# Linear attention for both halves of a supertile in one go, two PSUM tiles in other banks, and another DMA rate in the planner

## The chip, the cores and the metric

One Trainium2 chip, one of its cores. The metric is the device time of one execution in microseconds (us). TensorE is called PE here, VectorE DVE, ScalarE ACT, GpSimd POOL and SyncE SP, as in the profile.

## The reference

One decoder layer on 4096 tokens of width 1024: a modulated RMSNorm gives h, one projection of h feeds three kinds of heads (banded attention, RWKV-7, gated linear attention), their gated outputs go through one output projection, a second norm and the residual. The change touches the linear attention:

```python
def _gla_mixer(h, q, k, v, gk1, gk2, gk_b, norm_w):
    gk = jax.nn.log_sigmoid(((h @ gk1) @ gk2 + gk_b).astype(f32)) / GLA_GATE_NORMALIZER
    ...
    def step(S, inp):
        q_c, k_c, v_c, g_c = inp
        b = jnp.cumsum(g_c, axis=2)
        diff = b[:, :, :, None, :] - b[:, :, None, :, :]
        diff = jnp.where(causal[:, :, None], diff, -jnp.inf)
        A = jnp.einsum('bhid,bhjd,bhijd->bhij', q_c, k_c, jnp.exp(diff))
        o = A @ v_c + jnp.einsum('bhid,bhdv->bhiv', q_c * jnp.exp(b), S)
        b_last = b[:, :, -1:, :]
        S = (jnp.exp(b_last[:, :, 0, :])[..., None] * S
             + jnp.einsum('bhjd,bhjv->bhdv', k_c * jnp.exp(b_last - b), v_c))
        return S, o
    ...
    o = o * lax.rsqrt(jnp.mean(o * o, axis=-1, keepdims=True) + 1e-5) * norm_w.astype(f32)
```

There are 4 heads with keys of 32 and values of 64.

## The kernel before, in words

The tokens are cut into 16 supertiles of 256 (NT), each of two halves of 128 (a = 0, 1). Part one runs norm, RWKV-7 and linear attention over all supertiles and prepares the weights of part two; part two runs banded attention and the output projection.

Part one is written as streams of Python generators, one per stage and supertile: a (norm; xh are tokens by row, xt by column, rb the transposed row scales, hT the result in two f16 parts), p (projections pv, lp, zz, gqk), d (gates; here called w; its running sums of log decays are cw), qa, qb, qc (the 64-blocks' triangular inverse), v, k (transposes kp of the keys, copied to BK), q2 (the serial RWKV recurrence: rp, up, sp, yp in four steps per supertile, then yt), r (linear attention), c, g and l (weights: squares, scales, splits into two f16 parts; cs and ch).

Every instruction is also noted by `Order.note`. When a part has been emitted, `Order.pin` plays the instructions through its own table of costs, engine by engine, and chains each engine's instructions in the order that comes out. So a cost in that table, a buffer or a bank that an instruction must wait for, and a joint burst (matmuls noted as one group) all move instructions of every engine. On PE the planner prefers a ready matmul of the same array tile size. A load's end is set by its size class or, if later, by a pipe that moves 310 GB/s.

PSUM has eight banks of 128 x 512 f32: pj twice (projections), and one each of m, mq, at, tr, y and sq. `pst(tag, name)` takes a bank; a new tile in it waits for the readers of the last. In part one mq serves ktp, gap, kvp and ot of stage r, kp of stage k, and most of qa, qc and v; at serves atp, one half of np, bp and gap, and op; tr serves rb, aps and one cw; m serves the gates and the other cw.

Stage r per supertile: POOL spreads q over heads (qb, two tiles, one per half), PE transposes k (ktp, copied to kt by ACT). Then for each half: gap (keys by queries, 4 matmuls in array tiles of 64*64 into two banks), and DVE masks it back into qb. Then for each half: Gst, the state spread over heads, from the packed state Gpk (DVE), kvp (keys by values, 4 matmuls in tiles of 128*32), the next Gpk (two DVE instructions), op (state by queries, 2 matmuls, and masked products by values, 8, in tiles of 128*64), and ACT copies op to osb. Last a norm per head (squares in osq), transposes ot and a store.

Of the kernel before, what the change touches and what calls it, by code (L numbers as in the profile page):

```python
# [16 lines left out]
ALU = mybir.AluOpType  # L17
# [4 lines left out]
P = 128  # L22
D = 1024
T = 4096
NT = 256
NS = T // NT
KD = D // P
HD = 64
# [5 lines left out]
LIFT = {}  # L34
LAG = {"l": 150}
URGENT = 150
TILING_WAIT = 0.6
LANES = ((0.06, 1.04e-3, VL), (0.02, 1.0e-3, AL), (0.1, 2.3e-3, 0.0), (0.0, 1e-3 / 2.4, PL), (0.05, 0.0, 2.0))

# [24 lines left out]
class Order:  # L64
# [157 lines left out]
    def pin(self):  # L222
# [4 lines left out]
        for k, st in enumerate(steps):  # L227
            if st.eng == "PE":
                h = head[k - 1] if k else 0
# [13 lines left out]
        cells, mode, table, pipe, half = [0.0] * 16, None, None, 0.0, {}  # L243
        last, count = {}, 0
        while count < len(steps):
            e = min((e for e in ENGINES if ready[e]), key=lambda e: max(free[e], min(ready[e].values())))
            now = max(free[e], min(ready[e].values())) + 1e-9
            at = sorted((k for k, t in ready[e].items() if t <= now), key=lambda k: (steps[k].rank, k))
            k = at[0]
            if e == "PE" and mode is not None and steps[k].array[0] != mode:  # L250

                same = [q for q in at if steps[q].array[0] == mode]
                wait = max(now - ready[e][q] for q in at if steps[q].array[0] != mode)
                if same and (mode != (4, 4) or wait < TILING_WAIT):
                    k = same[0]
            first = max(free[e], ready[e].pop(k))
            for k in bursts.get(k, [k]):
                st, t = steps[k], max(first, free[e])
                if e == "PE":
                    m, at, passes, took, issue = st.array  # L260
                    if mode is not None and m != mode:
                        t = max(t, max(cells)) + 0.094
                    mode = m
                    t = max(t, max(cells[c] for c in at))
                    for c in at:
                        cells[c] = t + passes * took
                    free[e], st.end = t + issue * passes, t + passes * took + 0.165
                else:
                    if st.half is not None:
                        was, half[e] = half.get(e, st.half), st.half  # L270
                        if was[0] != st.half[0] or None not in (was[1], st.half[1]) and was[1] != st.half[1]:
                            t = max(t, free[e] + 0.115)
                    if st.table is not None and st.table != table:
                        t, table = max(t, free[e] + 1.28), st.table
                    free[e], st.end = t + st.occ, t + st.lat
                    if st.bytes:

                        pipe = max(pipe, t + 1.7) + st.bytes / 310e3
                        st.end = max(st.end, pipe)
                st.start = t  # L280
                if e in last:
                    self.tc.add_manual_dep(
                        st.ins, last[e], mybir.DependencyInfo(mybir.DependencyClass.NoSync, mybir.DependencyReason.DATA))
                last[e], count = st.ins.name, count + 1
                for q in st.then:
                    to, h = steps[q], head[q]
                    left[h] -= 1
                    at = t if k in to.turn else 0.0
                    if k in to.needs and e != to.eng:
                        at = max(at, st.end + HOP_FROM[e] + HOP_INTO.get(to.eng, 0.0))  # L290
                    elif k in to.needs and (e == "SP" or e != "PE" and to.needs[k]):
                        at = max(at, st.end + (0.05 if e == "SP" else 0.03))
                    when[h] = max(when[h], at)
                    if not left[h]:
                        ready[to.eng][h] = when[h]
# [105 lines left out]
def hybrid_kernel(ctx, tc, x, xc, rows, ada1, adaw, w1, wl, w2, wo, cst, abias, out):  # L401
# [72 lines left out]

    ps = pool_of(ctx, "ps", 1, space=PSUM)

    def pst(tag, name, bufs=1):
        bufs = 2 if tag == "pj" else bufs
        t = ps.tile([P, 512], F32, tag=tag, name=name, bufs=bufs)
        model.take(tag, bufs, t.tensor.name)  # L480
        return t
# [7 lines left out]
    def mq(name):  # L489
        return pst("mq", name)  # L490
# [45 lines left out]
    def joint(on=True):  # L536
        model.order.joint = next(burst) if on else 0
# [102 lines left out]
    with ExitStack() as p1:  # L640
# [1 line left out]
        soon = ("tables", "scolb", "uw", "w0p0", "w0p1", "one16", "mu_s", "mu_c", "a0h")  # L642
        late = ("td", "tf0", "tf1", "Sst0", "Sst1", "lnx")
        tags = ("gvh", "gvl", "xh", "b1", "gl", "bl", "cs", "ch", "gw", "zs", "gaw", "gacc", "zl0", "zl1", "zl2", "early",
                "zb1", "ta", "em", "ep", "zb0", "b2", "zb2", "kg", "kt", "egm", "egp", "qg", "vg", "c2", "middle",
                "AS", "osb", "c3", "KB", "ATm", "c1", "RA", "UV", "BK", "cd", "em0", "bon", "ysb", "rs", "Ss", "lasts")
        wk1 = {n: pool_of(p1, f"work1{n}", 1) for n in tags}

# [6 lines left out]
        def wt(shape, name, bufs=1, dt=F32, tag=None):  # L655
            tag = tag or name
            return wk1[tag].tile(shape, dt, tag=tag, name=name, bufs=bufs)
# [5 lines left out]
            return wt(shape, name, 3, dt, "b1")  # L663

        def cs2(shape, name, dt=F32):
            return wt(shape, name, 2, dt, "c2")

        def cs1(shape, name, dt=F32):
            return wt(shape, name, 4, dt, "c1")
# [708 lines left out]
        def stage_r(i):  # L1378
# [2 lines left out]
            yield [("p", i), ("r", i - 1)]  # L1381
            qg, kg, vg, egp, egm = e["qg"], e["kg"], e["vg"], e["egp"], e["egm"]
            half = (slice(0, 64), slice(64, 128))
            qb = [cs2([P, 4, P], "qb") for _ in range(2)]
            for a in range(2):
                G.tensor_tensor(qb[a], qg[:, a, :].rearrange("p (o n) -> p o n", o=1).to_broadcast([P, 4, P]),
                                bdm.rearrange("p (h n) -> p h n", h=4)[:, :, 0:1].to_broadcast([P, 4, P]), op=ALU.mult)
            yield [kg, "mq"]
            ktp = mq("ktp")
# [1 line left out]
                PE.transpose(ktp[:, a * P : (a + 1) * P], kg[:, a, :], ident)  # L1391
            kt = wt([P, 2, P], "kt", 1)
            S.copy(kt.rearrange("p a n -> p (a n)"), ktp[:, :NT])
            for a in range(2):
                yield [qb[a], "at", "mq"]
                gap = [pst(tag, "gap")[:, 0:NT] for tag in ("at", "mq")]
                joint()
                for hk in half:
                    for hp, sl in enumerate(half):
                        PE.matmul(gap[hp][hk], kg[sl, a, hk], qb[a][sl, 2 * hp : 2 * hp + 2, :].rearrange("p h n -> p (h n)"),  # L1400
                                  start=True, stop=True)
                joint(False)

                for hp in range(2):
                    V.tensor_tensor(qb[a][:, 2 * hp : 2 * hp + 2, :], gap[hp].rearrange("p (h n) -> p h n", h=2),
                                    gmask.rearrange("p (o n) -> p o n", o=1).to_broadcast([P, 2, P]), op=ALU.mult)
            yield [kt, "mq"]
            osb = wt([P, 2, NT], "osb", 1)
            for a in range(2):
                gidx = 2 * i + a  # L1410
                Gc, now, then = Gst[gidx % 2], Gpk[gidx % 2], Gpk[(gidx + 1) % 2]
                heads4 = [t.rearrange("p (h n) -> p h n", h=4) for t in (Gc, bdm)]
                V.scalar_tensor_tensor(heads4[0], now.rearrange("p (o n) -> p o n", o=1).to_broadcast([P, 4, HD]),
                                       egm[:, a, 0:1], heads4[1], op0=ALU.mult, op1=ALU.mult)
                kvp = mq("kvp")
                joint()
                for h in range(4):
                    PE.matmul(kvp[32 * h : 32 * h + 32, 0:HD], kt[:, a, 32 * h : 32 * h + 32], vg[:, a, h * HD : h * HD + HD],
                              start=True, stop=True)
                joint(False)  # L1420
                V.scalar_tensor_tensor(then, now, egm[:, a, 0:1], kvp[:, 0:HD], op0=ALU.mult, op1=ALU.add)
                V.tensor_scalar(then, then, egp[:, a, 128:129], None, op0=ALU.mult)
                yield [Gc, qb[a], "at"]
                op_ = pst("at", "op")
                joint()
                for ht in half:
                    PE.matmul(op_[ht, :NT], qg[:, a, ht], Gc, start=True, stop=False)
                for h in range(4):
                    for ht in half:
                        PE.matmul(op_[ht, h * 64 : h * 64 + 64], qb[a][:, h, ht], vg[:, a, h * 64 : h * 64 + 64],  # L1430
                                  start=False, stop=(h == 3))
                joint(False)
                S.copy(osb[:, a, :], op_[:, :NT])
                yield [then, "mq"]
            osq = cs2([P, 2, NT], "osq")
            gla_norm(osb, osq)
            yield [osb, "mq"]

# [126 lines left out]
                    (8, "a", stage_a, i), (9, "c", stage_c, i), (10, "p", stage_p, i))  # L1565
        emit()
        model.order.pin()


    def pool2(name):  # L1570
# [664 lines left out]
```

## Time and profile before

| | |
|---|---|
| median of 3 runs | 2021.44 us (2020.94 to 2027.34) |
| the profiled execution | 2023.94 us, span 2022.1 us |
| granted PE clock, mean | 0.989 |
| PE / DVE / ACT / POOL busy | 1919.5 / 1506.7 / 1130.1 / 311.3 us |
| part one | to about 1050 us: the last yt starts at 1038.4 us |
| part two | from 961.8 us (its first projection, kp from hT), beside the end of part one |

A row of the profile gives the line, engine, operation, out<-in by tile names and shapes. Nearly all rows read L336, the helper that issues and notes every instruction, so tiles tell them apart. A timeline row begins with start and duration; the bracket at its end is the engine's idle time before it and what released it. In a tile's view the three durations are smallest, median and largest in ns, and below them come two lists: what the tile's engine waited for, and who waited for the tile (us, times).

### The profile page before, as it was taken

Reading aid. Unit: us, or ns where it says so; the run is one execution under the profiler, and the core shown is the slowest. Engines: PE = TensorE matmul, PEld = TensorE weight load, DVE = VectorE, ACT = ScalarE, POOL = GpSimd, SP = SyncE. Lnnn points to the kernel's source line nnn. Section 1 sums busy time; section 2 is a strip of 40 time slices with the busy share of each in tenths; the row PEclk is TensorE's granted clock in tenths of the full one; section 3 lists DMA queues with packets and bytes.
Section 4 is the critical chain, followed back from the end, with each engine's and each line's share of the span. In section 5 each row is a group of like instructions: output and inputs, shape, how many; then the busy total and the mean of one; then the engine's idle time right before and its main releaser. Section 6 shows DMA issues by size and latency. Waiting matters only on the chain.

```text
span 2022.1 us, 59931 instructions
## 1 busy us (share of the span) xinstructions
PE 1919.5 (95%) x24899; PEld 1483.7 (73%) x24899; DVE 1506.7 (75%) x4246; ACT 1130.1 (56%) x2609; POOL 311.3 (15%) x485
## 2 busy tenths in 40 slices
PE   5899999999999999999989999999999999999997
PEld 1677787777787777877767678877778777787683
DVE  5777877887778887776758876777767777676866
ACT  5878778765866765555434544444454444444443
POOL 0622213262221222221100000000000000000001
PEclk8899999999999999999999999999999999999998
DMA  9464535353424411124243433344333443334414
GB/s 373 150 208 148 164 114 160 118 150 110 131 76 147 151 37 60 61 76 141 93 152 125 154 106 117 117 139 139 97 108 116 149 129 112 110 108 141 128 36 168
DMA packets 154267, 258.77 MB, mean 128 GB/s; under 512 B 49026, under 2 KB 100738, under 8 KB 147716
## 3 DMA queue, kind: packets, MB, share of 16 engines
q1 hardware_dynamic: 153844, 254.34, 38.8%
q8 instruction: 198, 3.24, 0.6%
q14 instruction: 81, 0.66, 0.1%
q10 hardware_dynamic: 144, 0.52, 0.1%
HBM read 193.98 MB, written 60.82 MB: 126 GB/s over the span
## 4 chain that ended last, share of the span: by engine, by line
PE 54%; DVE 22%; ACT 9%; DMA 8%; issue 4%; SPq 2%; POOL 1%; DVEq 0%; ACTq 0%; POOLq 0%
PE gp L336 16%; PE op L336 12%; PE zz L336 4%; PE qp L336 3%; PE pv L336 2%; PE lp L336 2%; PE kp L336 2%; PE sc L336 2%; DVE pr L336 2%; PE ovp L336 2%; DVE q L336 2%; DVE mtp L336 2%; SPq L336 2%; DMA cs<-in_wo 1%; DVE tsc L336 1%
## 5 line engine op out<-in xcount | busy, mean ns | idle before, releaser
L336 PEld LDWEIGHTS <-mtp 128*128 128x128 f16 x1344 | 130.7, 98 | 146.0 <-issue 6.3
L336 PE MATMUL op<-o,mtp 128*128 128x512 f16 x768 | 172.9, 380 | 0.0
L336 ACT ACTIVATE pr<-pr,nm,lsc 128x256 f32<-128x256 f32 (+1 forms) x256 | 149.0, 584 | 11.5 <-DVE nm L336 11.4
L336 PE MATMUL op<-ov,mtp 128*128 128x512 f16 x576 | 144.0, 381 | 3.6 <-DMA ov<-woscr 3.5
L336 PEld LDWEIGHTS <-hT 128*128 128x128 f16 x1536 | 120.5, 100 | 24.5 <-issue 3.9
L336 ACT ACTIVATE mtp<-yv,oi 128x1024 f16<-128x1024 f32 x30 | 34.5, 1149 | 155.1 <-DVE yv L336 114.4
L336 DVE CUSTOM_DVE_ANT_0 pr<-sc,ab,kept 128x256 f32<-128x256 f32 (+1 forms) x256 | 108.4, 475 | 15.5 <-PE sc L336 15.2
L336 POOL TENSOR_TENSOR ry<-sy,expo 128x1 f32<-128x1 f32 x30 | 19.1, 638 | 588.3 <-DVE sy L336 588.3
L336 PE MATMUL pv<-gvh,hT 128*128 128x272 f16 x512 | 101.0, 290 | 5.6 <-ACT hT L336 2.6
L336 DVE TENSOR_TENSOR yv<-op,yv 128x512 f32<-128x512 f32 x105 | 70.3, 681 | 47.3 <-PE op L336 33.4
L336 DVE SCALAR_TENSOR_TENSOR ag<-ag,gp 128x512 f32<-128x512 f32 x64 | 43.4, 678 | 67.8 <-ACT ag L336 67.7
L336 PE MATMUL zz<-hT,rh 128*128 128x256 f16 x512 | 91.8, 277 | 1.7 <-DVE x L336 1.7
L336 PE MATMUL lp<-hT,Lh 128*128 128x256 f16 x512 | 91.3, 274 | 1.7 <-issue 1.6
L336 PE MATMUL zz<-hT,kh 128*128 128x256 f16 x512 | 91.9, 273 | 0.0
L336 ACT ACTIVATE ag<-gp,gh 128x512 f32<-128x512 f32 x64 | 43.9, 686 | 83.3 <-PE gp L336 83.3
L336 PE MATMUL qp<-hT,q1h 128*128 128x256 f16 x512 | 86.3, 273 | 3.7 <-DVE kT L336 3.7
L336 PE MATMUL zz<-hT,vh 128*128 128x256 f16 x512 | 89.4, 275 | 0.0
L336 PE MATMUL gqk<-hT,gqkh 128*128 128x256 f16 x512 | 87.5, 273 | 1.1 <-DVE zb L336 1.1
L336 PE MATMUL gp<-hT,q5h 128*128 128x256 f16 x512 | 86.3, 273 | 0.0
L336 PE MATMUL qp<-hT,q0h 128*128 128x256 f16 x512 | 85.4, 273 | 0.0
L336 PE MATMUL gp<-hT,q3h 128*128 128x256 f16 x512 | 85.3, 273 | 0.0
L336 PE MATMUL gp<-hT,q6h 128*128 128x256 f16 x512 | 85.2, 273 | 0.0
(442 smaller groups left out, 5858.5 us busy)
## 6 DMA issues: line engine op xcount, KB each, us to landing
ov<-woscr SPq DMA_DIRECT2D x96, 512.0 KB, 4.5
xh<-in_x SPq DMA_DIRECT2D x32, 512.0 KB, 4.2
xt<-in_xc SPq DMA_DIRECT2D x16, 1024.0 KB, 8.3
hscr<-hT SPq DMA_DIRECT2D x16, 1024.0 KB, 5.0
hT<-hscr SPq DMA_DIRECT2D x16, 1024.0 KB, 4.8
x<-in_x SPq DMA_DIRECT2D x30, 512.0 KB, 4.3
out<-yv SPq DMA_DIRECT2D x30, 512.0 KB, 3.0
cs<-in_w SPq DMA_DIRECT2D x56, 256.0 KB, 3.5
```

Of the source, the lines that this page charges most:

```text
L336: r = f(*args, **kw)
```

## The change

Three edits. First, stage r treats both halves together: one qb tile, gap as one burst of 8 matmuls into two banks and two masks of 128x512 for both halves, kvp as one burst of 8, then the two state updates on DVE, then op as one burst of 20 in one bank and one copy to osb. Second, in part one kp takes the bank tr instead of mq, and the cw that took m takes at. Third, the planner's pipe moves 400 GB/s instead of 310. The buffers of the tag c2 go from two to one, and osq has a tag of its own.

```diff
+HOME = {('kp', 'mq'): 'tr', ('cw', 'm'): 'at'}
...
-                        pipe = max(pipe, t + 1.7) + st.bytes / 310e3
+                        pipe = max(pipe, t + 1.7) + st.bytes / 400e3
...
+    first_phase = [True]
+
     def pst(tag, name, bufs=1):
+        tag = HOME.get((name, tag), tag) if first_phase else tag
...
         def cs2(shape, name, dt=F32):
-            return wt(shape, name, 2, dt, "c2")
+            return wt(shape, name, 1, dt, "c2")
...
-            qb = [cs2([P, 4, P], "qb") for _ in range(2)]
+            qb = cs2([P, 2, 4, P], "qb")
...
+            yield [qb, "at", "mq"]
+            gap = [pst(tag, "gap").rearrange("p (a n) -> p a n", a=2) for tag in ("at", "mq")]
+            joint()
             for a in range(2):
-                yield [qb[a], "at", "mq"]
-                gap = [pst(tag, "gap")[:, 0:NT] for tag in ("at", "mq")]
-                joint()
                 for hk in half:
                     for hp, sl in enumerate(half):
-                        PE.matmul(gap[hp][hk], kg[sl, a, hk], qb[a][sl, 2 * hp : 2 * hp + 2, :].rearrange("p h n -> p (h n)"),
+                        PE.matmul(gap[hp][hk, a], kg[sl, a, hk], qb[sl, a, 2 * hp : 2 * hp + 2, :].rearrange("p h n -> p (h n)"),
                                   start=True, stop=True)
-                joint(False)
-
-                for hp in range(2):
-                    V.tensor_tensor(qb[a][:, 2 * hp : 2 * hp + 2, :], gap[hp].rearrange("p (h n) -> p h n", h=2),
-                                    gmask.rearrange("p (o n) -> p o n", o=1).to_broadcast([P, 2, P]), op=ALU.mult)
+            joint(False)
+            for hp in range(2):
+                V.tensor_tensor(qb[:, :, 2 * hp : 2 * hp + 2, :], gap[hp].rearrange("p a (h n) -> p a h n", h=2),
+                                gmask.rearrange("p (a o n) -> p a o n", a=1, o=1).to_broadcast([P, 2, 2, P]), op=ALU.mult)
             yield [kt, "mq"]
+            kvp = mq("kvp")[:, 0 : 2 * HD].rearrange("p (a n) -> p a n", a=2)
+            joint()
+            for a in range(2):
+                for h in range(4):
+                    PE.matmul(kvp[32 * h : 32 * h + 32, a], kt[:, a, 32 * h : 32 * h + 32], vg[:, a, h * HD : h * HD + HD],
+                              start=True, stop=True)
+            joint(False)
...
-                V.scalar_tensor_tensor(then, now, egm[:, a, 0:1], kvp[:, 0:HD], op0=ALU.mult, op1=ALU.add)
+                V.scalar_tensor_tensor(then, now, egm[:, a, 0:1], kvp[:, a], op0=ALU.mult, op1=ALU.add)
                 V.tensor_scalar(then, then, egp[:, a, 128:129], None, op0=ALU.mult)
-                yield [Gc, qb[a], "at"]
-                op_ = pst("at", "op")
-                joint()
+            yield [*Gst, qb, "at"]
+            op_ = pst("at", "op").rearrange("p (a n) -> p a n", a=2)
+            joint()
+            for a in range(2):
                 for ht in half:
-                    PE.matmul(op_[ht, :NT], qg[:, a, ht], Gc, start=True, stop=False)
+                    PE.matmul(op_[ht, a], qg[:, a, ht], Gst[(2 * i + a) % 2], start=(a == 0), stop=False)
...
-                S.copy(osb[:, a, :], op_[:, :NT])
-                yield [then, "mq"]
-            osq = cs2([P, 2, NT], "osq")
+            joint(False)
+            S.copy(osb, op_)
+            osq = wt([P, 2, NT], "osq")
...
         model.order.pin()
+        first_phase.clear()
```

How the order of PE moves at stage r. Before, in the ninth supertile, around the second half's kvp and op (up, sp and yp are the recurrence, zz a projection):

```order
L336 MATMUL zz<-hT,rh 128x256
L336 MATMUL up<-rs,tf_526 64x64 x4
L336 MATMUL kvp<-vg,kt 32x64 x4
L336 MATMUL op<-Gst_505,qg 64x256 x2
L336 MATMUL op<-vg,qb 64x64 x8
L336 MATMUL sp<-UV,BK 64x64 x4
L336 MATMUL yp<-UV,AT 64x64 x4
```

The same supertile after the change, first around kvp, then around op:

```order
L337 MATMUL sp<-UV,BK 64x64 x4
L337 MATMUL yp<-UV,AT 64x64 x4
L337 MATMUL kvp<-vg,kt 32x64 x8
L337 LDWEIGHTS kh
L337 MATMUL zz<-hT,kh 128x256
```

```order
L337 MATMUL zz<-hT,kl 128x256
L337 MATMUL op<-Gst_507,qg 64x256 x2
L337 MATMUL op<-vg,qb 64x64 x8
L337 MATMUL op<-Gst_508,qg 64x256 x2
L337 MATMUL op<-vg,qb 64x64 x8
L337 MATMUL sp<-UV,BK 64x64 x4
L337 MATMUL yp<-UV,AT 64x64 x4
```

There is one kvp burst and one op burst per supertile, further apart than before; the recurrence's matmuls stand at both.

How the order of ACT moves between 52 and 67 us of the span, where it squares the tokens of the second supertile (xh) and splits the weights r, v and gqk. Before:

```order
L336 ACTIVATE ch,wss_720<-cs 128x512 x2
L336 ACTIVATE rh<-stg,wsc 128x1024 x2
L336 ACTIVATE xh,ssx<-xh 128x1024
L336 ACTIVATE vh,wss_586<-stg 128x1024
L336 ACTIVATE vh,wss_586<-stgRA 128x1024
L336 ACTIVATE bl<-lp,ivL 128x256
L336 ACTIVATE vh<-stg,wsc 128x1024
L336 ACTIVATE vh<-stgRA,wsc 128x1024
L336 ACTIVATE gqkh,wss_611<-stgUV 128x1024
L336 ACTIVATE gqkh,wss_611<-stgKB 128x1024
L336 ACTIVATE xh,ssx<-xh 128x1024
```

After:

```order
L337 ACTIVATE xh,ssx<-xh 128x1024
L337 ACTIVATE rh<-stg,wsc 128x1024 x2
L337 ACTIVATE ch,wss_723<-cs 128x512
L337 ACTIVATE vh,wss_589<-stg 128x1024
L337 ACTIVATE vh,wss_589<-stgRA 128x1024
L337 ACTIVATE xh,ssx<-xh 128x1024
L337 ACTIVATE bl<-lp,ivL 128x256
L337 ACTIVATE ch,wss_723<-cs 128x512
L337 ACTIVATE vh<-stg,wsc 128x1024
L337 ACTIVATE vh<-stgRA,wsc 128x1024
L337 ACTIVATE gqkh,wss_614<-stgUV 128x1024
L337 ACTIVATE gqkh,wss_614<-stgKB 128x1024
```

Both squares of xh have moved ahead of the weights that they stood behind, and one of two squares of cs behind the weights r.

The order of DVE in the same stretch, from the second split of v on (wtot, p2e and wsc are the scale of gqk, zlT the copy of zp). Before:

```order
L336 SCALAR_TENSOR_TENSOR vl<-stgRA,wsc,vh 128x1024
L336 TENSOR_REDUCE wtot<-wssp 128x1
L336 TENSOR_SCALAR p2e<-wtot 128x1
L336 TENSOR_SCALAR p2e<-p2e 128x1
L336 TENSOR_SCALAR msx<-ssx 128x2
L336 TENSOR_SCALAR p2e<-p2e 128x1
L336 COPY zlT<-zp 17x256
L336 TENSOR_SCALAR p2f<-p2e 128x1
L336 TENSOR_SCALAR p2e<-p2e 128x1
L336 TENSOR_SCALAR wsc<-p2f 128x1
L336 TENSOR_SCALAR ivgqk<-p2e 128x1
L336 TENSOR_SCALAR ivgqk<-ivgqk,hinv 128x1
```

After:

```order
L337 SCALAR_TENSOR_TENSOR vl<-stgRA,wsc,vh 128x1024
L337 TENSOR_TENSOR xt<-xt,rb 128x1024 x2
L337 TENSOR_REDUCE wtot<-wssp 128x1
L337 TENSOR_SCALAR p2e<-wtot 128x1
L337 TENSOR_SCALAR p2e<-p2e 128x1 x2
L337 COPY zlT<-zp 17x256
L337 TENSOR_SCALAR p2f<-p2e 128x1
L337 TENSOR_SCALAR p2e<-p2e 128x1
L337 TENSOR_TENSOR hT<-xt,hT 128x512
L337 TENSOR_SCALAR wsc<-p2f 128x1
```

Both products xt<-xt,rb of the second supertile now stand ahead of wtot and zlT; before they came behind them.

More of the change, by code (lines that the diff above doesn't have):

```diff
@@ L644, in hybrid_kernel @@
         tags = ("gvh", "gvl", "xh", "b1", "gl", "bl", "cs", "ch", "gw", "zs", "gaw", "gacc", "zl0", "zl1", "zl2", "early",
-                "zb1", "ta", "em", "ep", "zb0", "b2", "zb2", "kg", "kt", "egm", "egp", "qg", "vg", "c2", "middle",
+                "zb1", "ta", "em", "ep", "zb0", "b2", "zb2", "kg", "kt", "egm", "egp", "qg", "vg", "c2", "osq", "middle",
                 "AS", "osb", "c3", "KB", "ATm", "c1", "RA", "UV", "BK", "cd", "em0", "bon", "ysb", "rs", "Ss", "lasts")
@@ L1383, in stage_r @@
             half = (slice(0, 64), slice(64, 128))
-            qb = [cs2([P, 4, P], "qb") for _ in range(2)]
+            qb = cs2([P, 2, 4, P], "qb")
             for a in range(2):
-                G.tensor_tensor(qb[a], qg[:, a, :].rearrange("p (o n) -> p o n", o=1).to_broadcast([P, 4, P]),
+                G.tensor_tensor(qb[:, a], qg[:, a, :].rearrange("p (o n) -> p o n", o=1).to_broadcast([P, 4, P]),
                                 bdm.rearrange("p (h n) -> p h n", h=4)[:, :, 0:1].to_broadcast([P, 4, P]), op=ALU.mult)
@@ L1414, in stage_r @@
                                        egm[:, a, 0:1], heads4[1], op0=ALU.mult, op1=ALU.mult)
-                kvp = mq("kvp")
-                joint()
[L1417 to L1420, printed above, removed]
-                V.scalar_tensor_tensor(then, now, egm[:, a, 0:1], kvp[:, 0:HD], op0=ALU.mult, op1=ALU.add)
+                V.scalar_tensor_tensor(then, now, egm[:, a, 0:1], kvp[:, a], op0=ALU.mult, op1=ALU.add)
                 V.tensor_scalar(then, then, egp[:, a, 128:129], None, op0=ALU.mult)
-                yield [Gc, qb[a], "at"]
-                op_ = pst("at", "op")
-                joint()
+            yield [*Gst, qb, "at"]
+            op_ = pst("at", "op").rearrange("p (a n) -> p a n", a=2)
+            joint()
+            for a in range(2):
                 for ht in half:
-                    PE.matmul(op_[ht, :NT], qg[:, a, ht], Gc, start=True, stop=False)
+                    PE.matmul(op_[ht, a], qg[:, a, ht], Gst[(2 * i + a) % 2], start=(a == 0), stop=False)
                 for h in range(4):
                     for ht in half:
-                        PE.matmul(op_[ht, h * 64 : h * 64 + 64], qb[a][:, h, ht], vg[:, a, h * 64 : h * 64 + 64],
-                                  start=False, stop=(h == 3))
-                joint(False)
-                S.copy(osb[:, a, :], op_[:, :NT])
-                yield [then, "mq"]
-            osq = cs2([P, 2, NT], "osq")
+                        PE.matmul(op_[ht, a, h * 64 : h * 64 + 64], qb[:, a, h, ht], vg[:, a, h * 64 : h * 64 + 64],
+                                  start=False, stop=(h == 3 and a == 1))
+            joint(False)
+            S.copy(osb, op_)
+            osq = wt([P, 2, NT], "osq")
             gla_norm(osb, osq)
```

## The prediction

> **What bounds the kernel now.** I read the page first, then the stretches of the span by engine, then TensorE's order of time at the places that the change touches.
>
> ```profile
> span 2022.1 us, 59931 instructions
> ...
> PE 1919.5 (95%) x24899; PEld 1483.7 (73%) x24899; DVE 1506.7 (75%) x4246; ACT 1130.1 (56%) x2609; POOL 311.3 (15%) x485
> ...
> PE 54%; DVE 22%; ACT 9%; DMA 8%; issue 4%; SPq 2%; POOL 1%; DVEq 0%; ACTq 0%; POOLq 0%
> ```
>
> TensorE (PE) is busy for 95% of the span and is the largest part of the chain that ended last. An average over stages is not enough, so here are the stretches. The columns are the stretch, its length, the busy time (and instructions) of PE, PEld, DVE, ACT and POOL, the granted clock, the DMA share and GB/s.
>
> ```profile
> 0.00:40.00 40.00, 19.80 (x78) 4.78 (x78) 18.06 (x92) 15.98 (x29) 3.10 (x18) 0.96 0.97 377
> 40.00:100.00 60.00, 47.69 (x405) 37.46 (x405) 45.72 (x110) 53.43 (x103) 32.80 (x41) 0.84 0.55 183
> 100.00:1050.00 950.00, 912.06 (x14755) 735.05 (x14753) 731.33 (x2296) 628.51 (x1388) 243.24 (x379) 0.99 0.39 122
> 1050.00:1200.00 150.00, 142.49 (x1502) 107.25 (x1503) 116.86 (x288) 70.22 (x176) 6.48 (x7) 1.00 0.38 123
> 1200.00:1950.00 750.00, 738.80 (x7744) 564.68 (x7743) 547.62 (x1364) 333.78 (x857) 19.72 (x35) 1.00 0.37 120
> 1950.00:2022.00 72.00, 58.67 (x422) 34.50 (x419) 47.16 (x100) 28.14 (x61) 6.01 (x6) 0.92 0.37 126
> ```
>
> Part one runs to about 1050 us. Its first 40 us are set by the loads (DMA share 0.97), the next 60 us lean on ACT (53.43 of 60.00). From 100 to 1050 us PE idles 950.00 - 912.06 = 37.9 us, so PE bounds part one too: a change there is worth the PE time that it removes plus whatever it does to these 37.9 us. In part two, 1200 to 1950 us, PE idles 11.2 us of 750; the change adds nothing there but the planner's new DMA rate, which shifts six matmul rows per supertile among their neighbours. I cost part two at nothing; what hides it is that PE has a next projection matmul at every place, and if that cover failed the 11.2 us show the scale.
>
> **Array reconfigurations, the main term.** The tile size in the array (128*128, 64*64, ...) stands in each row of PE's timeline. A change of tile size costs time by itself:
>
> ```profile
> 559.05 0.27 PE L336 MATMUL lp<-hT,Ll 128*128 128x256 f16 x1
> 559.16 0.27 PE L336 MATMUL lp<-hT,Lh 128*128 128x256 f16 x1
> 559.36 0.75 PE L336 MATMUL Xp<-D,ATm 32*32 32x32 f32 x64
> 560.05 0.28 PE L336 MATMUL lp<-hT,Lh 128*128 128x256 f16 x1
> ...
> 560.27 0.38 PE L336 MATMUL lp<-hT,Lh 128*128 128x256 f16 x2
> 560.49 0.27 PE L336 MATMUL lp<-hT,Ll 128*128 128x256 f16 x1
> 560.60 0.38 PE L336 MATMUL lp<-hT,Lh 128*128 128x256 f16 x2
> 560.91 0.78 PE L336 MATMUL Xq<-td,Xs 32*32 32x32 f32 x64
> ```
>
> Two 128x256 matmuls take 0.22 us from start to start where the tile size stays (560.27 to 560.49), and 0.31 where it changes next (560.60 to 560.91); one takes 0.11 (559.05 to 559.16) against 0.20 (559.16 to 559.36). Leaving the small tiles costs the same: a matmul normally starts 0.16 before the one ahead of it ends (559.05 + 0.27 against 559.16), after the Xp burst it starts 0.06 before its end (560.11 against 560.05). So 0.09 to 0.10 us for each change of tile size. Counted over all matmuls up to the last yt burst of part one, the order holds 693 changes before and 641 after: gap, kvp and op come in 16 bursts each instead of 32, and fewer of them stand alone between projections. 52 x 0.09 = 4.7 us, all of it on PE and so on the path. The matmuls themselves are the same in number and shape.
>
> **Linear attention for both halves: waits and other engines.** The first four rows are from the views of the tiles qb, kvp and osb (a row with two numbers is who waited: us, times), then the cost of the same shapes elsewhere, then the state's steps.
>
> ```profile
> L336 DVE TENSOR_TENSOR qb<-gap,masks x64: 412/416/425, 117.3 to 986.0; 128x256 f32<-128x256 f32 x64
>   PE op L336: 2.1, 2
>   PE kvp L336: 1.2, 1
> L336 ACT COPY osb<-op x32: 352/372/416, 125.1 to 993.4; 128x256 f32<-128x256 f32 x32
> L336 DVE TENSOR_TENSOR AT<-atp,masks 128x512 f32<-128x512 f32 x64 | 41.2, 683 | 19.8 <-PE atp L336 19.7
> 34.50 0.59 ACT L336 COPY adrow<-adp 128x512 f32<-128x512 f32 x1 [12.46 <-PE adp L336]
> L336 DVE SCALAR_TENSOR_TENSOR Gpk<-Gpk,egm,kvp x32: 264/272/281, 123.4 to 992.8; 128x64 f32<-128x64 f32 x32
> L336 DVE TENSOR_SCALAR Gpk<-Gpk,egp x32: 221/247/256, 123.8 to 993.2; 128x64 f32<-128x64 f32 x32
> L336 DVE SCALAR_TENSOR_TENSOR Gst<-Gpk,egm,kept x31: 455/477/486, 124.6 to 991.6; 128x256 f32<-128x256 f32 x31
> ```
>
> DVE: 64 masks of 416 ns become 32 of 128x512, by the AT row 683 ns: 26.6 - 21.9 = 4.8 us less. ACT: 32 copies of 372 ns become 16 of some 590: 11.9 - 9.4 = 2.5 us less. Neither is on the path (DVE busy 77% from 100 to 1050 us, ACT 66%), the projections cover both, so I credit 0; with that cover gone they would be worth 7.3 us at the very most. POOL's qb products, the transposes and the stores stay as they are, in number. qb has one buffer for both halves now, so the next supertile's products wait for this one's op; they come a supertile later (950 us by 16 is 59 us), which covers that.
>
> PE's own idle before this stage's matmuls is 2.1 (op) + 1.2 (kvp) = 3.3 us. With half as many bursts I take half of it away, 1.7 us; the ends are 0 and 3.3. Against it stands a new wait: op for the first half can no longer go ahead of kvp, since all of op now waits for the state after the first half, that is Gpk 272 + Gpk 247 + Gst 477 = 1.0 us of DVE work behind the merged kvp. Queued behind a waiting op on PE would be the recurrence's sp and yp and all projections. In the order at least 18 matmuls lie between kvp and op (14 or more of them projections, in 15 of the 16 supertiles), some 1.5 us at 0.11 each, so I add 0 and keep the other end for a rival.
>
> **Other banks.** kp leaves the bank mq for tr, one cw leaves m for at.
>
> ```profile
>   PE kp L336: 1.3, 3
>   DMA xh<-in_x: 15.8, 9
> ```
>
> PE waited 1.3 us for its own kp to be copied out; both kp still share one bank, so that wait stays. Freed mq may let other bursts go earlier, and tr now has kp ahead of rb, aps and cw. No row prices the exchange. I bound it by the same 1.3 us to either side and take 0, since every burst keeps projections to hide behind.
>
> **The planner's 400 GB/s.** Nothing in the data moves faster; the order changes. The load-bound start moved 408 GB/s from 40 to 46 us and 377 over the first 40:
>
> ```profile
> 40.00:46.00 6.00, 2.93 (x12) 1.67 (x12) 5.24 (x15) 4.96 (x12) 0.00 (x0) 0.50 1.03 408
> 60.00:80.00 20.00, 14.92 (x120) 11.21 (x119) 15.14 (x40) 16.96 (x30) 11.90 (x15) 0.83 0.33 101
> ```
>
> So 400 is nearer to what a burst does than 310. SP's issues up to 50 us keep their order, and the first 40 us I leave unchanged. The Trainium skill, "DMA: Bandwidth & Descriptors", section Specifications, speaks against it: it gives about 358 GB/s as a core's share of HBM. By that figure 400 errs as far as 310 did, and nothing would be gained by it; the 408 GB/s above differ from the page, for one core running alone.
>
> The order does change between 50 and 100 us, where ACT now squares the second supertile's tokens (xh) before the weights r, and DVE does both xt products before it answers zp and the sums of gqk:
>
> ```profile
> 65.60 0.38 PE L336 MATMUL wssp<-wss,first 128*128 128x2 f32 x2 [2.54 <-ACT gqkh L336]
> 67.22 0.65 PE L336 MATMUL gp<-kept,zlT 17*64 17x128 f32 x8 [0.59 <-DVE p2f L336]
> 70.15 0.58 PE L336 MATMUL zz<-hT,rh 128*128 128x256 f16 x2 [1.71 <-DVE x L336]
> 94.17 0.66 PE L336 MATMUL kp<-first,KB 128*128 128x128 f32 x4 [1.96 <-DVE KB L336]
> 96.22 0.39 PE L336 MATMUL pv<-gvh,hT 128*128 128x272 f16 x1 [1.40 <-DVE zb L336]
> 66.76 0.40 DVE L336 COPY zlT<-zp 17x256 f32<-17x256 f32 x1
> 68.48 1.22 DVE L336 TENSOR_TENSOR xt<-xt,rb 128x1024 f32<-128x1024 f32 x1 [0.44 <-PE rb L336]
> 69.62 0.48 DVE L336 SCALAR_TENSOR_TENSOR x<-lp,ivL,bl 128x256 f32<-128x256 f32 x1
> ```
>
> Two products of 1.22 us ahead of zlT can hold gp up by 2.4 us (and x, which frees the bank that zz waits for): that is the loss end. With the second supertile's hT done sooner, the waits of 1.71, 1.96 and 1.40 us can go: 5.1 us, the gain end. Both have their cause in the same rows; I take the middle, -1.3.
>
> **Sum.** -4.7 - 1.7 - 1.3 = -7.7 us. The profiled execution took 2023.94 us (span 2022.1); less 7.7 that is 2016.2. It lies 2.5 us above the median of the three runs, 2021.44, against which the change is timed, so 2013.7, called 2014. What no row decides is how PE's other waits fall in the new order: 37.9 us in some 70 pieces of half a microsecond; if each is drawn anew with a spread like its size (0.7), the sum moves by about 6 us. This is an estimate.
>
> **Rivals.** What this kernel's timing can tell from no change is about 0.3%, 6 us.
>
> (a) The changes of tile size go, but PE then waits where it used to reconfigure: the start loses its 2.4 us and the stage's waits stay, -4.7 + 2.4 = -2.3, 2019 us. For it: 641 is the planner's doing, and its plan already missed by 37.9 us. Against it: fewer bursts are fewer places to miss.
>
> (b) Slower: the merged op catches up with DVE. Place: PE, at the op burst of each of the 16 supertiles. Price: 1.0 us of state work plus one 1.2 us product ahead of it in DVE's queue, less the cover. It decides from (7.7 + 6.1) / 16 = 0.86 us of wait per supertile on; at 1.0 us each the time is 2014 + 16 = 2030. Against it: the 18 matmuls between.
>
> (c) Loads come later than the new plan holds, and ACT, in order, blocks on them. ACT already waits 15.8 us for xh in 9 waits. At 358 instead of 400 GB/s a 512 KB load is 0.15 us late and a 1 MB one 0.31; over 32 and 16 loads that is 9.8 us, and if all of it reached PE, 2024. That is the rate of the page named above. The 408 GB/s in the row speak against it.
>
> (d) A larger gain: the start's idle vanishes and with it PE's half clock. From 60 to 80 us the clock is 0.83, which is 6.8 us at half speed, worth 3.4 us; with the 5.1 us of waits instead of 1.3 the time is 2014 - 3.8 - 3.4 = 2007. The Trainium skill, "TensorE: Matmul & The Clock Gate", Part 1, says that an idle window of about 3.4 us halves the clock until a busy one; the trace agrees in the length of that stretch, which is two such windows. Against (d): the wssp wait of 2.54 us stays in the order.
>
> **How the numbers follow.** The forecast 2014: 0.50; (d): 0.06; (a): 0.32; (c): 0.04; (b): 0.08. Faster by over 0.3% (under 2015.4) is the forecast and (d): 0.56; within 0.3% is (a) and (c): 0.36; slower is (b): 0.08. Low end: 2021.4 - 4.7 - 3.3 - 5.1 - 6 = 2002.3, called 2003. High end: 2021.4 - 4.7 + 2.4 + 6 = 2025.1, called 2025. (b) lies outside.
>
> **What would show it.** Right: DVE's qb masks 32 times near 683 ns, osb copies 16 times; PE's busy time in part one down by about 5 us at unchanged matmul counts; PE's idle from 100 to 1050 us not above 38 us; part two's supertiles as long as before. Wrong: op or sp waiting for Gst in most supertiles; more ACT idle on xh or cs; zz or gp waiting longer than 2.5 us near 65 to 72 us; or the PE idle total moving by more than the 4.7 us that the tile sizes give.

## The result, and the profile after

The changed kernel took 2011.08 us (median of 5 runs, 2009.07 to 2016.8) against 2021.44 us: a ratio of 0.9942, 95% interval 0.9927 to 0.9957, or some 10 to 12 us faster. That lies 3 us under the forecast of 2014 and inside its range. The experiments show that the number came out for other reasons than the ones given: the merged stage r brought nothing, the other banks brought about twice the whole gain, and the 400 GB/s gave half of that away.

The page of the changed kernel's profiled execution (2012.25 us): its span, the busy time of the engines, and the shares of the chain that ended last.

```profile
span 2010.2 us, 59878 instructions
...
PE 1909.2 (95%) x24899; PEld 1481.8 (74%) x24899; DVE 1503.7 (75%) x4214; ACT 1131.7 (56%) x2593; POOL 306.6 (15%) x485
...
PE 54%; DVE 21%; DMA 9%; ACT 8%; issue 4%; SPq 2%; POOL 1%; DVEq 0%; ACTq 0%; POOLq 0%
```

TensorE is busy 10.3 us less with the same 24,899 matmuls. Its waits by stretches, from the view by windows of the changed kernel (start and end, length, then busy time and count of PE, PEld, DVE, ACT and POOL, the clock, DMA share and GB/s):

```profile
0.00:40.00 40.00, 20.83 (x78) 4.73 (x78) 18.77 (x93) 16.13 (x29) 3.10 (x18) 1.00 0.97 380
40.00:100.00 60.00, 48.54 (x444) 38.53 (x445) 48.06 (x109) 53.52 (x103) 31.30 (x40) 0.86 0.54 181
100.00:1050.00 950.00, 908.08 (x14838) 737.92 (x14836) 733.99 (x2282) 631.83 (x1380) 241.20 (x380) 0.99 0.39 123
```

From 100 to 1050 us TensorE now idles 41.9 us, before 37.9, though the kernel is faster: equal times are not equal work. So from here on part one is compared over the same 16,525 matmuls. The two kernels' windows that hold them, before and after:

```profile
0.00:1175.00 1175.00, 1097.92 (x16525) 865.80 (x16526) 893.85 (x2737) 755.27 (x1665) 285.00 (x443) 0.99 0.42 134
```

```profile
0.00:1165.00 1165.00, 1089.29 (x16525) 864.25 (x16526) 890.97 (x2705) 755.77 (x1649) 280.30 (x443) 0.99 0.42 135
```

Ten microseconds are gained here, 8.6 of them busy time and 1.4 idle time (77.1 to 75.7). What follows takes 847 us before and 845 after.

### The profile page after: what moved, and what is told of

It is laid out like the page before. It is cut to its first block, busy times and chain, and to the rows that moved or that the text cites. A ratio compares the mean times of both kernels' runs of the same rounds, so it can differ in the third digit from the quotient of the medians.

```text
span 2010.2 us, 59878 instructions
## 1 busy us (share of the span) xinstructions
PE 1909.2 (95%) x24899; PEld 1481.8 (74%) x24899; DVE 1503.7 (75%) x4214; ACT 1131.7 (56%) x2593; POOL 306.6 (15%) x485
## 4 chain that ended last, share of the span: by engine, by line
PE 54%; DVE 21%; DMA 9%; ACT 8%; issue 4%; SPq 2%; POOL 1%; DVEq 0%; ACTq 0%; POOLq 0%
PE gp L337 16%; PE op L337 12%; PE zz L337 4%; PE qp L337 4%; SPq L337 2%; PE pv L337 2%; PE lp L337 2%; PE kp L337 2%; PE sc L337 2%; DVE q L337 2%; DVE mtp L337 2%; PE ovp L337 2%; DMA cs<-in_w 2%; DVE pr L337 2%; PE gqk L337 1%
## 5 line engine op out<-in xcount | busy, mean ns | idle before, releaser
L337 PE MATMUL gp<-hT,q4h 128*128 128x256 f16 x512 | 85.9, 273 | 0.0
```

Source lines behind the costliest of these rows:

```text
L337: r = f(*args, **kw)
```

## The experiments

The change has three parts, and each was tried alone and with the others. Theories, under the names that the expectations use: **T1**, the prediction's own (fewer changes of the tile size through the merged stage r); **T2**, each edit draws the planner's order anew and this one was lucky; **T3**, the 400 GB/s help through the start; after the first four runs also **B** (the banks are a real gain) and **D** (the higher rate does harm). Each expectation's "before" is the kernel before on the same chip, whose median was 2021.9, 2024.1 and 2022.2 us in the three groups of runs.

**The merged stage r alone.**

```
-HOME = {('kp', 'mq'): 'tr', ('cw', 'm'): 'at'}
+HOME = {}
...
-                        pipe = max(pipe, t + 1.7) + st.bytes / 400e3
+                        pipe = max(pipe, t + 1.7) + st.bytes / 310e3
```

> The merged stage r alone; the banks and the 310 GB/s are as before. Part one's order has 663 changes of the tile size on TensorE (before 693, after 641). Theory T1, the time follows the tile-size changes: 30 fewer at 0.09 us are -2.7 us, and the waits before op and kvp fall from 3.5 us to under 1 us as in the changed kernel (-2.5), so 2016 us, about 5 us under before, and a busy time of TensorE about 3 us lower. Theory T2, the gain is a lucky drawing of the whole order (half-clock stretches and waits elsewhere): anything from 2015 to 2027, with TensorE's busy time changed by the half-clock stretches alone. Theory T3, the gain comes with the rate of 400 GB/s through the start: no change, 2020 to 2022.

Measured: 2021.14 us, ratio 0.9995 (0.9982 to 1.0008). No gain; T1 expected 2016. The profiled execution, at 2017.21 us, is the second fastest of its twelve, so its 5 us less of idle time (72.0 against 77.1 us in part one) may not be typical of the kernel.

**The banks alone**, in the kernel before (HOME as in the change, stage r and 310 GB/s as before).

> The two other PSUM banks alone (kp in tr, cw in at). 688 changes of the tile size in part one's order. T1: 5 fewer at 0.09 us, -0.5 us, so 2021, no difference. T2: a new drawing of the order, off by up to 6 us either way. T3: 2020 to 2022.

Measured: 1999.21 us, ratio 0.9887 (0.9872 to 0.9901), 23 us faster and twice the gain of the whole change. T1 expected no difference, T2 at most 6 us either way. The same matmuls of part one, banks alone:

```profile
0.00:1150.10 1150.10, 1092.44 (x16525) 865.86 (x16526) 885.84 (x2737) 754.38 (x1665) 281.80 (x443) 0.99 0.43 137
```

Against before, TensorE is busy 5.5 us less and idle 57.7 instead of 77.1 us: 19.4 us of waits are gone, four times the 3.3 and 1.3 us that stood in the prediction's rows on r and kp.

**The rate alone** (400 for 310 GB/s in the kernel before).

> The planner's rate alone, 400 for 310 GB/s. 690 changes of the tile size in part one's order. T1: -0.3 us, 2021. T2: off by up to 6 us either way. T3: most of the 10 us of the changed kernel, 2011 to 2014, and already there by the seventh supertile, at about 350 us.

Measured: 2034.76 us, ratio 1.0063 (1.0046 to 1.0081), 13 us slower. T3 falls, with the wrong sign. Part one with the rate alone; idle 84.8 us:

```profile
0.00:1188.00 1188.00, 1103.19 (x16525) 867.43 (x16526) 897.42 (x2737) 755.46 (x1665) 278.13 (x443) 0.99 0.41 133
```

**Merged stage r and banks, without the rate.** The changed kernel with `310e3` in the line of the pipe.

> The changed kernel with the planner's rate back at 310 GB/s: the merged stage r and the banks. 641 changes of the tile size in part one's order, as many as in the changed kernel. T1: as fast as the changed kernel within 3 us, 2010 to 2014. T2: off from it by up to 6 us either way. T3: back at 2019 to 2022.

Measured: 2002.65 us, ratio 0.9908 (0.9892 to 0.9924): 7 us faster than the whole change. T1 and T3 miss, and so does T2, which allowed 6 us; the banks stay a gain and the merge adds none. Part one; idle 65.1 us:

```profile
0.00:1155.30 1155.30, 1090.17 (x16525) 866.05 (x16525) 886.63 (x2705) 753.54 (x1649) 277.70 (x443) 0.99 0.42 136
```

**One bank at a time**, in the kernel before.

```
+HOME = {('kp', 'mq'): 'tr'}
```

> Only the keys' transposes go to the other bank (kp in tr); cw stays in m, stage r and the rate as before. 683 changes of the tile size in part one's order. Theory B (a real gain of the banks, through the crowded bank mq): kp is the one name that leaves mq, the bank of wssp, gap, kvp, ktp, ot, Xp, Xq, X2, vp, yt and half of np, bp and atp, so nearly all of the 22.7 us that the two banks gave: 1999 to 2004, with TensorE's idle time 15 to 20 us lower than before. Theory T2 (the drawing of the order alone): any edit draws again, 2000 to 2034. Theory T1 (tile-size changes, 0.09 us each): -0.9, 2020 to 2021.

Measured: 2008.66 us, ratio 0.9933 (0.9907 to 0.996). B's bound of 2004 was missed, and so was its 15 to 20 us less of idle time (65.2 us in part one, 11.9 less than before), but the larger piece of the gain is here.

```
+HOME = {('cw', 'm'): 'at'}
```

> Only half of the running sums go to the other bank (cw in at instead of m). 712 changes of the tile size in part one's order. Theory B through mq: nothing of the gain, 2016 to 2022; B through m (gp, zp, wps and cgp wait less): the gain of 22.7 us is here, under 2005. T2: 2000 to 2034. T1: +1.7, 2023.

Measured: 2036.65 us, ratio 1.0065 (1.0043 to 1.0087): alone this half does harm, outside what any form of B had and just outside T2's 2034. The two do not add up: -0.67% and +0.65% alone, -1.13% together. So moving cw seems to pay only when kp has moved as well; why is open, and the 0.46% that it then adds is not far above what a redrawn plan moves (next runs).

**Plans drawn again**: 340 GB/s, nothing else, in the kernel before and with the banks.

> The kernel before with the planner's rate at 340 instead of 310 GB/s: a plan drawn again, with nothing else in it. 717 changes of the tile size in part one's order. B: 2018 to 2035, no gain beyond some us, since the banks are as before. T2: a spread of 10 us or more either way, so a value under 2012 would speak for T2 and against B. A real harm by a higher rate (theory D: 400 GB/s gave +12.9): between, about 2025. T1: +2.2, 2024.

> The two other banks with the planner's rate at 340 GB/s. 684 changes of the tile size in part one's order. B: within 6 us of the 1999 that the banks gave at 310 GB/s, so under 2006. T2: anything from 2000 to 2034. D (the rate harms by itself): 2003. T1: 2020.

Measured: 2027.79 us (1.0023, 1.0008 to 1.0037) without the banks, 1997.61 us (0.9859, 0.9835 to 0.9884) with them. T2 would let these overlap, and they lie 30 us apart. D's 2025 is near the first and its 2003 misses the second, which came out a little faster than at 310 GB/s.

**The rest of the table**: banks with 400 GB/s, merge with 400 GB/s, and the changed kernel at 340 GB/s.

> The two other banks and the planner's 400 GB/s, stage r as before. 688 changes of the tile size in part one's order, as with the banks at 310 GB/s. Theory B (the banks are worth some 24 us, and each drawing of the order moves the time by some 6 us about that): 1993 to 2010. Theory D (400 GB/s in the plan harms by itself, by the 8 to 13 us of its two pairs so far): 2007 to 2012, above both of its neighbours at 310 and 340 GB/s (1999 and 1998).

> The merged stage r and the planner's 400 GB/s, without the other banks. 669 changes of the tile size in part one's order. B: without kp's new bank it stays at 2018 to 2035. D: 2029 to 2034. T1 (merged r is a gain by itself against 2034.8 with the rate alone): 2029, and the busy time of r's matmuls (op, gap, kvp) again about 6 us under the unmerged kernels', as in the three merged profiles so far.

> The changed kernel with 340 GB/s in the plan. 643 changes of the tile size in part one's order. B with drawings: 1993 to 2010. D: 2002 to 2004, between 310 (2002.7) and 400 (2011.1). T1 (the merge is a gain where the drawing is the same kind): 3 to 5 us under the unmerged one at 340 GB/s, 1993 to 1995; if the merge's shorter busy time is always given back in waits, 1997 to 2003.

Measured: 2009.26 us (0.9931, 0.9907 to 0.9955); 2035.51 us (1.0072, 1.0048 to 1.0096); 2009.43 us (0.9931, 0.991 to 0.9952). D holds in the first; B, with 1993 to 2010, holds there too. The second is slower than the merge alone, as D has it, but lies 1.5 us above D's 2034 and 0.5 above B's 2035; T1's 2029 is missed. At 340 GB/s the merged kernel is slower than the unmerged one by 0.7%, where T1 wanted it faster and D wanted it at 2002 to 2004; B's 1993 to 2010 holds.

All eight combinations, medians in us and ratios to before:

| | r as before, 310 | r merged, 310 | r as before, 400 | r merged, 400 |
|---|---|---|---|---|
| banks as before | 2021.9, 1 | 2021.1, 0.9995 | 2034.8, 1.0063 | 2035.5, 1.0072 |
| other banks | 1999.2, 0.9887 | 2002.7, 0.9908 | 2009.3, 0.9931 | 2011.1, 0.9942 |

Each part has four pairs that differ in it alone. Banks: -1.13, -0.87, -1.32 and -1.30%, mean -1.16%, 23 us. Rate: +0.63, +0.77, +0.44 and +0.34%, mean +0.55%, 11 us. Merge: -0.05, +0.09, +0.21 and +0.11%, mean +0.09%, 2 us, hardly more than nothing; the pair at 340 GB/s has +0.72% and would make the mean +0.22%, 4 us. Their sum, -0.52%, is close to the -0.58% of the change. The redraws at 340 GB/s moved the time by +0.23, -0.28 and +0.23% against 310 GB/s, some 5 us either way. So a redrawn order moves the time, but little beside the banks: the seven kernels with kp in tr and the usual planner lie at 1998 to 2011 us, the six with kp in mq at 2021 to 2037.

**Fewer changes of the tile size, by the planner alone.** With the banks only, the planner may hold back a ready step of another tile size for longer while whole-array matmuls are there:

```
-TILING_WAIT = 0.6
+TILING_WAIT = 3.0
```

> The two other banks at 310 GB/s, with the planner holding back a ready step of another tile size for up to 3.0 us instead of 0.6 while whole-array matmuls are there. 634 changes of the tile size in part one's order against 688 with the banks alone. T1: 54 fewer at 0.09 to 0.12 us, TensorE's busy time 5 to 6 us lower, and 1993 to 1995 if nothing waits for the steps held back. Rival: the recurrence is held back and TensorE waits for it later, so busy lower by 5 us and idle higher by 5 or more, 1999 to 2008.

Measured: 2132.95 us, ratio 1.0543 (1.0519 to 1.0566): 134 us slower than the banks alone, with 54 fewer changes. The rival had the direction of the time, and was far too small. The same matmuls, and the longest groups of TensorE's waits (engine, tile, releaser: us in total, times, longest):

```profile
0.00:1289.10 1289.10, 1148.68 (x16525) 901.69 (x16526) 905.67 (x2737) 752.03 (x1665) 273.80 (x443) 0.94 0.38 122
```

```profile
PE ot L337 <- DVE osb L337: 12.1, 8, 4.1
PE Xp L337 <- DVE AT L337: 8.1, 3, 4.8
PE vp L337 <- ACT ysb L337: 8.1, 4, 2.6
PE rp L337 <- DVE Ss L337: 6.9, 9, 1.8
```

Idle time rises from 57.7 to 140.4 us: the chain of small steps (Xp, rp, ot) was what had been held back, and in the end TensorE waits for it. Busy time rises too, by 56 us, because of the clock (last section). It is not a clean price of a tile-size change, but it shows that holding steps back for fewer changes can cost far more than it saves.

## Why the prediction was right in its number and wrong in its reasons

**Array reconfigurations, the main term (-4.7).** In its place it happened. The view by windows restricted to one tile, from 100 us to the end of part one's matmuls: gap, kvp and op before, then after (op's rows hold 168 matmuls of part two's op as well, in both kernels).

```profile
100.00:1175.00 1075.00, 22.63 (x256) 8.26 (x256) 25.07 (x64) 0.99 0.39 122
100.00:1175.00 1075.00, 10.21 (x256) 5.03 (x256) 8.73 (x32) 0.99 0.39 122
100.00:1175.00 1075.00, 73.08 (x808) 27.01 (x640) 9.35 (x14) 12.97 (x34) 0.99 0.39 122
```

```profile
100.00:1165.00 1065.00, 19.14 (x256) 10.40 (x256) 21.10 (x32) 1.00 0.39 124
100.00:1165.00 1065.00, 7.06 (x256) 4.40 (x256) 8.73 (x32) 1.00 0.39 124
100.00:1165.00 1065.00, 70.13 (x808) 25.89 (x640) 9.35 (x14) 10.36 (x18) 1.00 0.39 124
```

The same matmuls take 3.5, 3.2 and 3.0 us less. Records overlap; counting only what no earlier matmul covers, and time at half clock as half, the three fall from 94.7 to 88.9 us, and in the four pairs that differ in the merge alone by 5.9, 7.7, 6.0 and 6.0 us. This saving does not follow the count of changes: the merge takes away 30 of 693 by itself, 21 of 690 with the rate and 47 of 688 with the banks. So the 52 were in part the redrawn plan's, and 0.09 us as the price of each is not confirmed. The step that failed is the next one, "all of it on PE and so on the path". With the banks, the merge lowered part one's busy time by 2.3 us at 310 GB/s and raised its idle time by 7.4 (57.7 to 65.1); at 400 GB/s it was 2.9 and 5.6 (from windows of 1092.23 busy in 1162.3 us to those above). Little of that was at stage r itself (0.5 us at op and 0.7 at kvp that were not there before); most fell on other steps of the chain, the largest rises here. From the view of waits, banks alone and then merge with banks, 310 GB/s:

```profile
PE yt L337 <- DVE ysb L337: 4.3, 4, 2.2
...
PE rp L337 <- DVE Ss L337: 0.5, 1, 0.5
PE ktp L337 <- DVE bon L337: 0.4, 1, 0.4
```

```profile
PE yt L337 <- DVE ysb L337: 6.2, 8, 2.3
PE rp L337 <- DVE Ss L337: 2.5, 3, 1.2
PE ktp L337 <- DVE bon L337: 2.4, 5, 1.0
```

Without the banks the one profiled execution of each kernel shows another way to lose it: idle time fell, by 5.1 and 2.0 us, but matmul time at half clock rose, from 26.2 to 32.8 us and from 27.8 to 36.7. So the matmuls of stage r saved about what was forecast (6 for 4.7 us), and its worth to the end was about zero. Rival (a) had named this mechanism (TensorE then waits where it used to reconfigure); its 2019 us did not come, since the banks moved the time elsewhere.

**Waits of stage r (-1.7).** Right in place: the changed kernel's waits before op and kvp in part one are

```profile
PE op L337 <- DVE Gst L337: 0.7, 1, 0.7
...
PE op L337 <- DMA ov<-woscr: 0.4, 1, 0.4
...
PE kvp L337 <- DVE qb L337: 0.2, 1, 0.2
```

of which the middle one belongs to part two's op. 3.3 us became 0.9, and the new wait for the state came once, so the 0 credited for it stands and rival (b) does not occur. Like the term above, it did not shorten the kernel by itself (0.9995).

**DVE and ACT off the path (0).** The counts and sizes came as said, from the views of qb and osb after:

```profile
L337 DVE TENSOR_TENSOR qb<-gap,masks x32: 672/681/693, 111.0 to 972.8; 128x512 f32<-128x512 f32 x32
L337 ACT COPY osb<-op x16: 564/579/587, 121.4 to 977.8; 128x512 f32<-128x512 f32 x16
```

Some 7 us less work on the two engines, and no gain from the merge: off the path, as assumed.

**Other banks (0, at most 1.3 either way).** The largest error: -23 us. The step that failed is "I bound it by the same 1.3 us to either side". The wait of kp for its own copy-out is no bound on what a freed bank is worth; probably it is only what the old order left in place, since the planner had already put everything else around the bank mq (this is an argument, not a measurement). TensorE's whole idle time in part one was 77.1 us. In the four pairs, in the order given above, the banks took 19.4, 6.8, 14.7 and 7.1 us of idle time, and 5 to 14 us of busy time, which no row of waits shows. Which tile's wait shrinks differs from plan to plan. That most of the gain needs kp out of mq is shown by its run alone and by the gap between the two groups of kernels; the path by which the planner uses the free bank is not shown.

**The planner's 400 GB/s (-1.3, ends -5.1 and +2.4).** Wrong in sign and size: +11 us. The start is hardly where it acts: the first thousand matmuls end at 144.0 us before, 143.9 after and 145.5 with the rate alone, though a wait of the loss end's size, 2.6 us, did come (at zp, not at gp). In the timeline of the changed kernel's TensorE and DVE:

```profile
65.70 0.38 PE L337 MATMUL wssp<-wss,first 128*128 128x2 f32 x2 [2.79 <-ACT gqkh L337]
68.68 0.61 PE L337 MATMUL zp<-first,vg 128*17 128x128 f32 x2 [2.60 <-DMA cs<-in_w]
66.22 2.34 DVE L337 TENSOR_TENSOR xt<-xt,rb 128x1024 f32<-128x1024 f32 x2
68.48 0.15 DVE L337 TENSOR_REDUCE wtot<-wssp 128x1 f32<-128x2 f32 x1
```

The view names a load as zp's releaser, but zp starts 0.05 us after the end of wtot, which before the change released it as well (after 0.25 us of idle time), and wtot now stands behind the two products, as the loss end had it.

The rate was judged by a burst of loads (408 GB/s in the start's 6 us). In the steady part each load of xt is issued 0.4 to 0.9 us behind a store of the same size, hscr. From the view of DMA of the kernel before (KB each, median us from issue to landing), then one such place in SP's timeline:

```profile
xh<-in_x SPq DMA_DIRECT2D x32, 512.0 KB, 4.2
xt<-in_xc SPq DMA_DIRECT2D x16, 1024.0 KB, 8.3
hscr<-hT SPq DMA_DIRECT2D x16, 1024.0 KB, 5.0
```

```profile
350.71 0.36 SPq L336 DMA_DIRECT2D hscr<-hT  x1
351.12 0.43 SPq L336 DMA_DIRECT2D xt<-in_xc  x1
```

By the planner's line the store takes 1.7 us and its bytes, and the load its own bytes behind them: with 1,048,576 bytes each and 0.41 us between the issues, xt lands 8.1 us after its issue at 310 and 6.5 at 400 GB/s, against 8.3 measured. So 310 was about right there, and 400 lets the plan count on xt some 1.8 us too early. (For 256 and 512 KB that stand alone the planner's size classes, 2.6 and 3.5 us, are later than its pipe at either rate, so there the edit changes nothing.) ACT's waits for loads, before and with the rate alone, from 100 to 1175 us:

```profile
ACT ch L336 <- DMA cs<-in_wo: 16.7, 12, 3.4
ACT xh L336 <- DMA xh<-in_x: 15.8, 9, 3.5
ACT ch L336 <- DMA cs<-in_w: 8.5, 10, 2.3
```

```profile
ACT ch L336 <- DMA cs<-in_w: 26.2, 18, 3.8
ACT xh L336 <- DMA xh<-in_x: 22.5, 13, 3.1
ACT ch L336 <- DMA cs<-in_wo: 17.9, 16, 3.1
```

41.0 us became 66.6. With ch's waits for woscr, the sums at 310 GB/s are 43, 55, 47 and 43 us, and at 400 GB/s 72, 58, 61 and 65. This is rival (c), loads later than the plan with ACT blocked on them, which got 0.04. It fits the four pairs in sign and not in size (with the merge alone, 3.7 us more of ACT's waits and 0.77% more time), so (c) as the cause is made likely and not shown; a rate under 310 would have tested it and was not run, and 340 GB/s, between the two, gave no steady rise (+0.23, -0.28 and +0.23%).

**Part two (0) and the redraw (6 us).** Right: after part one the eight kernels take 845 to 847 us, and the plans drawn again differ by about 5 us; that the forecast met 2011 within 3 us is luck all the same (next). Rival (d) did not come: the wait for gqkh stayed, with 2.79 us.

**The sum.** -4.7 - 1.7 + 0 - 1.3 came to -7.7, and the parts measured are about +2, -23 and +11. Errors of -23 and of +12 and +8 cancelled. Of the signs named beforehand, the sizes of DVE's and ACT's work and the lower busy time (8.6 us for some 5) came; TensorE's idle time from 100 to 1050 us, 41.9 us, passed the 38 allowed, over slightly more matmuls.

**A better version.** The banks without the merge and without 400 GB/s, at 1999.2 us and, with 340 GB/s, at 1997.6 us, beat both kernels: their ratios to before, 0.9887 and 0.9859, have intervals that do not touch that of the changed kernel, 0.9942.

## What to carry to other kernels

Where a planner writes the order, the wait that an edit's own row shows is no bound on what the edit is worth: the engine's whole idle time in that part is a better scale, and busy time can move too. Try each part of a bundle alone, since three parts here were worth +2, -23 and +11 us and the sum said nothing of that. Check a planner's rate for transfers against what the steady part's transfers take, queued as they are there, and not against the best burst; here the burst's 400 GB/s cost 11 us, by a path that was made likely and not shown. Busy time saved on the bounding engine is saved only if the chain of small dependent steps moves up with it.

## What the runs showed of the hardware

A stretch of TensorE that is only partly idle can be enough to halve its clock. From the windows of the kernel that holds other tile sizes back:

```profile
363.90:367.30 3.40, 3.40 (x55) 2.66 (x47) 2.31 (x4) 3.40 (x9) 0.00 (x0) 1.00 0.29 77
367.30:370.70 3.40, 1.93 (x66) 1.28 (x65) 2.95 (x6) 3.12 (x8) 0.37 (x2) 1.00 0.50 198
370.70:374.10 3.40, 3.29 (x16) 2.31 (x17) 1.67 (x5) 1.22 (x3) 0.37 (x2) 0.50 0.98 292
374.10:377.50 3.40, 3.40 (x61) 2.89 (x60) 0.34 (x1) 0.12 (x1) 0.00 (x0) 0.99 0.70 287
```

After 3.4 us with 1.93 us of matmuls the clock is 0.50 for the next 3.4 us, with TensorE busy. In that kernel's part one 24 of 25 such stretches follow 3.4 us with at most 2.05 us of matmuls (the other, 2.71). The Trainium skill, "TensorE: Matmul & The Clock Gate", Part 1, says that an idle window of about 3.4 us halves the clock; the runs agree in the length, and differ in that the window need not be wholly idle. So waits that bunch are paid twice: 121.5 us of matmul time ran at half clock there against 27.9 with the banks alone, and half of the difference, 47 us, is most of the 56 us by which its busy time rose.
